# Pools change places at the seam between projection and mixing, and one head's loads change queue

## The chip, the core and the metric

The kernel runs on one core of a Trainium2 chip. The metric is the device time of one execution in microseconds; three runs of a kernel give a median. The traces come from one profiled execution. TensorE (PE) multiplies matrices, VectorE (DVE), ScalarE (ACT) and GpSimd (POOL) work on tiles, SyncE (SP) issues most DMAs. Each engine takes its instructions strictly in the order in which they stand in its own program and waits on semaphores where one depends on another engine or on a DMA.

## What is computed

One layer of a streaming encoder is run for two request groups with the same weights: 1024 first frames of a new stream, and 32 further frames of a running one, which the kernel puts side by side into 1056 columns. Cut to what matters:

```
mod = silu(c) @ w_ada + b_ada                      # adaLN: shift, scale, gate
h = x * (1 + sc1) + sh1
mq,mk,mv,mo,mi,mf, fq,fk,fv,ff, gu,gv = split(h @ w_in)
hm = head_norm(mlstm(mq, mk, mv, ...)) * norm_g * sigmoid(mo)
hf = softmax(fq @ fk.T + decay(ff), causal) @ fv   # 8 heads of 64
hg = spatial_gate(gu, layer_norm(gv))
mix = concat([hm, hf, hg]) @ w_o
x = layer_norm(ALPHA * x + (1 + g1) * mix) * ln1_g + ln1_b
h = x * (1 + sc2) + sh2
y = (silu(h @ w_gate) * (h @ w_up)) @ w_down       # D_FF = 2816
x = layer_norm(ALPHA * x + (1 + g2) * y)
```

The softmax of a new stream runs over its whole past; the running stream brings a cache of 256 keys per head.

## The kernel before

**Arithmetic.** Products are taken in fp32 accuracy from rounded halves: each operand is split into a high part and a low remainder, and a product is three matmuls, high by high, high by low, low by high (`gemm`, L110). `weights` (L92) brings a weight block into `raw` by SP's queue, ScalarE makes the high half (L104, `whi`), VectorE the low one (L105, `wlo`).

**Columns and stages.** Model columns 0 to 511 are group 0, the rest group 1. Phase 1 projects everything and writes q, k, v, gates and so on to scratch arrays in DRAM (`dqh`, `dql`: high and low halves of q and k of each head; `dv`, `dmqk`, `dmv`, `dmo`; `dfs`: the forget decay; `dM`). Group 0's attention is done in phase 1. Then come group 0's output projection (`wo`), its first layer norm (`ln1`) and, for the last three heads, group 1's q and k (`fm_unit` with `evac_qk(h, True)`). In `evac_qk` (L358) ScalarE and VectorE write the halves into the small tiles `qkh` and `qkl`, SP stores them to `dqh` and `dql`, and the exact k goes from `qkr` to the output `o_kT` on ScalarE's own DMA queue. `ln1_res(0)` (L1094) rescales the residual `z[0]` on GpSimd (L1101), 16 tiles.

**The seam.** After that two pools are released (`s1.close()`): `p1`, with group 1's projection input in halves (`h1h`, `h1l`) and some constants, and `sm`, with the small tiles. Both lie on the right side of the on-chip memory; `sm` was opened second. The pool `mx1` is opened on the same side and takes their addresses. A tile of `mx1` may be written only when the last readers of what lay there are done; for a tile that was being stored, when the store has landed.

**What follows.** `mixers` (L1322) runs, for heads 0 to 7, the second phase of the attention (`fox`, L737: queries of tiles 4 to 7), woven with the mLSTM blocks (`mlstm`, L584; the first of them beside head 1 in the order of the program's text), and, before head 1, the running stream's attention (`fox_sample`). `fox` loads per head `qp` (q high and low), `k1` (k high, twice), `q2` and `k2` (with decay rows, `decay` L381) and `v`, all by SP's queue; the first two matmuls on them are L779 and L780 (`fox_s`). `mlstm` loads `mqk`, `mqb`, `mv1`, `mo` and `mb`; `mqb` and a column of `mv1` are first set by GpSimd (L594, L599); ScalarE then takes the sigmoid of `mo` in three steps (L607 to L609) and VectorE reads `mb` (L615). The feed-forward part of group 0 is written behind the mixers: `up` (L1122) multiplies the normed columns (`tm_ah`, `tm_al`) by gate and up weights into `up_g` tiles, takes silu in three ScalarE steps (L1139 to L1141) and two VectorE products (L1142, L1143) and splits the result. Pieces of adaLN (`ada`, L170: products L178, a copy by ScalarE L181, transposes L184, a sum L186) stand between.

**What sets the order.** The program's text is only the start: when the kernel is built, a scheduler that simulates a timeline puts the instructions into their final order on each engine, keeping dependencies, and interleaves `up`, `ada` and `mixers`. `issue_after(x)` forbids an instruction to be placed ahead of x.

Of the kernel before, what the change touches and what calls it, by code (L numbers as in the profile page):

```python
# [63 lines left out]
def f(ap):  # L64
    return ap.bitcast(F32)


class Kernel:
# [12 lines left out]
        kw = {} if bufs is None else {"bufs": bufs}  # L81
        return pool.tile(shape, dt, tag=tag, name=f"{self.phase}_{tag}_{self.n}", **kw)

    def load(self, out, in_):
        self.lastload = self.nc.sync.dma_start(out, in_)
        return self.lastload

# [290 lines left out]
                    nc.gpsimd.tensor_copy(self.qks[:, h, :], kr[:, n - NS:n])  # L378
        return evac

    def decay(self, out, h, rows, tiles):  # L381
        j0, j1 = tiles
        self.load(f(out).rearrange("p (j q) -> p j q", q=P),
                  self.dfs.rearrange("(j h) r q -> h r j q", h=8)[h, rows, j0:j1])

    def head_tiles(self, h, nq, nk):
        b = self.foxbufs
# [349 lines left out]
    def fox(self, h, chunks):  # L737
        self.phase = "fox"
        mx = self.mx
        q0, q1 = chunks[0][0] * P, (chunks[-1][-1] + 1) * P  # L740
        nq, nk, nb = q1 - q0, q1, q1 // P
        if h in self.heads:
            k1, k2, qp, q2, v = self.heads.pop(h)
        else:
            k1, k2, qp, q2, v = self.head_tiles(h, nq, nk)
            qs = slice(q0, q1)
            self.load(f(qp[0:64]), self.dqh[h, 0:64, qs])
            self.load(f(qp[64:128]), self.dql[h, 0:64, qs])
            self.load(f(k1[0:64]), self.dqh[h, 64:128, :nk])
            self.load(f(k1[64:128]), self.dqh[h, 64:128, :nk])  # L750
            self.load(f(q2[0:64]), self.dqh[h, 0:64, qs])
            self.decay(q2[64:68], h, slice(2, 6), (chunks[0][0], nb))
            self.load(f(k2[0:64]), self.dql[h, 64:128, :nk])
            self.decay(k2[64:68], h, slice(0, 4), (0, nb))
            self.load(f(v), self.dv[:, :nb, h * P:(h + 1) * P])
        for tiles in chunks:
            o = tiles[0] * P - q0
            n = len(tiles) * P
            yield from self.fox_chunk(h, tiles, nk, n, k1, k2, qp[:, o:o + n], q2[:, o:o + n], v)
# [405 lines left out]
    def sup_operand(self, ks):  # L1165
# [7 lines left out]
        def load(k):  # L1173
# [5 lines left out]
            return x, y  # L1179

        loaded = {k: load(k) for k in ks[:2]}
        yield
        for k in ks:
            self.phase = "sup"
            x, y = loaded.pop(k)
            tt(y[:, b], y[:, b], x[:, b], ALU.subtract)
            tt(x[:, b], x[:, a], x[:, b], ALU.subtract)
            tt(x[:, a], y[:, b], x[:, a], ALU.add)
            tt(y[:, a], x[:, a], y[:, a], ALU.subtract)
            for z, (h, l) in zip((x, y), self.T):  # L1190
                nc.scalar.copy(h[:, k], z)
                tt(l[:, k], z, f(h[:, k]), ALU.subtract)
            if k + 2 in ks:
                loaded[k + 2] = load(k + 2)
            yield
# [141 lines left out]
    def run(self):  # L1337
        nc, tc, d = self.nc, self.tc, self.d
# [25 lines left out]
        self.constants()  # L1364
        self.ph = self.pool("ph")
        s1 = ExitStack()
        self.p1 = self.pool("p1", ctx=s1, side="right")
        self.sm = self.pool("sm", 2, ctx=s1, side="right")
        self.h1t = [self.wide_tiles(), [self.t(self.p1, [P, KT, GN[1]], F32R, x) for x in ("h1h", "h1l")]]
        self.hs = self.t(self.p1, [P, KT, 2 * NS], F32R, "hs")  # L1370
        self.G = self.t(self.p1, [P, 9, 16], F32, "G")
# [97 lines left out]
        weave(self.ln1(0, st, *MM[0][1]))  # L1469
        for h in range(PRE, 8):  # L1470
            self.fm_unit(w3[2 + h], self.evac_qk(h, True), (1,))
        self.ln1_res(0)
        s1.close()
        s4 = ExitStack()
        self.mx = self.pool("mx1", ctx=s4, side="right")
        self.foxbufs = (2, 1, 1, 1, 2)
        self.mixers()
        s5 = ExitStack()
        pa = self.pool("pa0", ctx=s5)
        self.pu, self.utag = self.pg, "gg"  # L1480
# [78 lines left out]
        for half, (a, b) in enumerate(LN[1][::-1]):  # L1559
# [6 lines left out]
            else:  # L1566
                h, l = (self.t(pb, [P, KT * 272], F32R, f"{x}{a}", 1) for x in ("ah", "al"))
# [117 lines left out]
```

## Time and profile before

| | us |
|---|---|
| runs, median (lowest to highest, three) | 1366.96 (1365.69 to 1368.74) |
| profiled execution | 1366.61 |
| span of its trace, first to last instruction | 1364.7 |
| mean granted TensorE clock | 0.995 of full speed |

The profile's page begins with the busy time of each engine. The granted clock tells at what share of full speed TensorE was allowed to run. In a timeline the columns are start, duration, engine, line, operation, output and inputs, tile shape, and in brackets the idle time ahead of it and what ended it; the names of DMAs that an engine issues stand under a queue (SPq, ACTq). The names in the trace carry the phase: `fox_qp` is head 0's qp here, `fm_qkr` the small tile of group 1's projection, `up_whi` a weight half, `start_dqh` a scratch array. The windows table gives for a stretch the busy time and count of PE, its weight loads, DVE, ACT and POOL, then the clock, the share of the 16 DMA engines that is busy, and GB/s.

### The profile page before, as it was taken

How to read it: one execution, taken by the hardware profiler on the slowest of the kernel's cores; microseconds unless marked ns; L12 is line 12 of the kernel's file. 1: busy time of each engine (PE TensorE's matmuls, PEld its weight loads, DVE VectorE, ACT ScalarE, POOL GpSimd, SP SyncE). 2: the span in 40 equal slices, each digit the busy share in tenths (PEclk: the TensorE clock that was granted, in tenths of full speed). 3: DMA queues.
4: the chain of work that ended last, by engine and by line, in shares of the span. 5: the costliest groups of instructions: out<-in, count | busy, mean ns of one | idle time of the engine just before them, and what ended most of it. 6: DMA issues, size and time to landing. Idle time of an engine off the chain costs nothing.

```text
span 1364.7 us, 25185 instructions
## 1 busy us (share of the span) xinstructions
PE 1330.3 (97%) x9434; PEld 1215.8 (89%) x9434; DVE 995.4 (73%) x2129; ACT 656.7 (48%) x1306; POOL 226.6 (17%) x263
## 2 busy tenths in 40 slices
PE   7999999999999899999999999999999999999996
PEld 4898889998989777888887888999999999999995
DVE  5545553679769667786776765678988988879777
ACT  3314454545536554545545354336664554645355
POOL 0202000053134200000000000373710000000341
PEclk9999999999999899999999999999999999999998
DMA  9765565547454765454344334574596758454321
GB/s 359 273 231 152 161 206 154 163 138 212 134 201 135 207 189 171 119 154 134 109 122 120 104 110 130 156 181 124 164 254 170 205 149 223 146 170 127 99 79 66
DMA packets 119289, 221.70 MB, mean 162 GB/s; under 512 B 18676, under 2 KB 62352, under 8 KB 119168
## 3 DMA queue, kind: packets, MB, share of 16 engines
q1 hardware_dynamic: 111936, 207.55, 48.9%
q0 software_dynamic: 6032, 11.94, 5.1%
q8 instruction: 74, 1.21, 0.4%
q10 hardware_dynamic: 1200, 0.62, 0.2%
q14 instruction: 47, 0.39, 0.1%
HBM read 188.13 MB, written 51.85 MB: 176 GB/s over the span
## 4 chain that ended last, share of the span: by engine, by line
PE 84%; DVE 7%; DMA 5%; ACT 2%; issue 1%; SPq 1%; POOL 1%; DVEq 0%; ACTq 0%
PE up_g L117 5%; PE up_g L118 5%; PE up_g L116 5%; PE dn_g L116 4%; PE dn_g L118 4%; PE dn_g L117 4%; PE tm_g L281 3%; PE tm_g L282 3%; PE tm_g L283 3%; PE sup_u L118 3%; PE sup_u L116 3%; PE sup_u L117 3%; PE fox_t L815 2%; PE sup_g L117 2%; PE sup_g L118 2%; PE sup_g L116 2%
## 5 line engine op out<-in xcount | busy, mean ns | idle before, releaser
L117 PE MATMUL up_g<-tm_al,up_whi 128*128 128x512 f32 (+1 forms) x384 | 141.0, 367 | 0.5 <-DVE tm_al L1092 0.5
L116 PE MATMUL up_g<-tm_ah,up_whi 128*128 128x512 f32 (+1 forms) x384 | 141.2, 369 | 0.2
L118 PE MATMUL up_g<-tm_ah,up_wlo 128*128 128x512 f32 (+1 forms) x384 | 140.5, 366 | 0.0
L1211 ACT CAST sup_whi<-sup_raw 128x1024 fp32r<-128x1024 f32 x54 | 56.0, 1048 | 90.3 <-PE dn_u L117 46.7
L116 PEld LDWEIGHTS up_g<-tm_ah,up_whi 128*128 128x128 f32 x384 | 72.7, 190 | 12.5 <-ACT tm_ah L1091 0.6
L117 PEld LDWEIGHTS up_g<-tm_al,up_whi 128*128 128x128 f32 x384 | 73.1, 190 | 11.1 <-DVE tm_al L1092 0.7
L118 PEld LDWEIGHTS up_g<-tm_ah,up_wlo 128*128 128x128 f32 x384 | 73.2, 191 | 10.7
L788 ACT ACTIVATE fox_p<-fox_s,fox_fmx 128x384 f32<-128x384 f32 (+2 forms) x96 | 55.1, 578 | 44.8 <-DVE fox_fmx L786 37.4
L104 ACT CAST up_whi<-up_raw 128x1024 fp32r<-128x1024 f32 x50 | 52.4, 1048 | 49.7 <-PE up_g L117 19.0
L1212 DVE TENSOR_TENSOR sup_wlo<-sup_raw,sup_whi 128x1024 fp32r<-128x1024 f32 x54 | 68.2, 1267 | 10.5 <-ACT sup_whi L1211 10.5
L1066 DVE SCALAR_TENSOR_TENSOR wo_z<-dn_g,start_mod,wo_z 128x512 f32<-128x512 f32 (+4 forms) x120 | 60.3, 521 | 20.1 <-PE dn_g L118 19.7
L105 DVE TENSOR_TENSOR up_wlo<-up_raw,up_whi 128x1024 fp32r<-128x1024 f32 x50 | 65.7, 1314 | 11.6 <-ACT up_whi L104 11.0
L116 PE MATMUL dn_g<-up_acth,dn_whi 128*128 128x512 f32 (+2 forms) x200 | 74.1, 371 | 0.0
L118 PE MATMUL dn_g<-up_acth,dn_wlo 128*128 128x512 f32 (+2 forms) x200 | 73.4, 367 | 0.0
L117 PE MATMUL dn_g<-up_actl,dn_whi 128*128 128x512 f32 (+2 forms) x200 | 72.9, 365 | 0.0
L820 ACT CAST fox_pth<-fox_t 128x512 fp32r<-128x512 f32 (+1 forms) x80 | 41.0, 545 | 59.5 <-PE fox_t L815 59.3
L104 ACT CAST dn_whi<-dn_raw 128x1024 fp32r<-128x1024 f32 (+1 forms) x44 | 42.7, 971 | 52.2 <-PE up_g L117 10.7
L783 DVE TENSOR_REDUCE fox_fmx<-fox_s 128x1 f32<-128x384 f32 (+2 forms) x96 | 52.7, 553 | 13.0 <-PE fox_s L780 11.8
L821 DVE TENSOR_TENSOR fox_ptl<-fox_t,fox_pth 128x512 fp32r<-128x512 f32 (+1 forms) x80 | 49.5, 631 | 14.5 <-ACT fox_pth L820 14.4
L105 DVE TENSOR_TENSOR dn_wlo<-dn_raw,dn_whi 128x1024 fp32r<-128x1024 f32 (+1 forms) x44 | 49.5, 1125 | 13.7 <-ACT dn_whi L104 13.2
L281 PE MATMUL tm_g<-tm_whi,start_h1h 128*128 128x256 f32 (+1 forms) x192 | 55.3, 288 | 1.7 <-ACT tm_vhl L711 1.7
L282 PE MATMUL tm_g<-tm_wlo,start_h1h 128*128 128x256 f32 (+1 forms) x192 | 55.1, 287 | 0.0
(667 smaller groups left out, 4806.8 us busy)
## 6 DMA issues: line engine op xcount, KB each, us to landing
up_raw<-w_gu SPq DMA_DIRECT2D x50, 512.0 KB
dn_raw<-w_dn SPq DMA_DIRECT2D x28, 512.0 KB
ada_late<-w_ada SPq DMA_DIRECT2D x24, 512.0 KB
sup_raw<-w_gu SPq DMA_DIRECT2D x20, 512.0 KB
start_dp<-w_gu SPq DMA_DIRECT2D x19, 512.0 KB
start_dp<-w_gu POOLq DMA_DIRECT2D x19, 512.0 KB, 7.5
wo_raw<-w_o SPq DMA_DIRECT2D x18, 512.0 KB
sup_raw<-start_dp SPq DMA_DIRECT2D x18, 512.0 KB
```

The costliest lines, as they stand in the source:

```text
L104: nc.scalar.copy(hi[:, :w], raw[:, :w])
L105: (eng or nc.vector).tensor_tensor(lo[:, :w], raw[:, :w], f(hi[:, :w]), ALU.subtract)
L116: nc.tensor.matmul(ps, hi, xh(k), start=start and k == 0, stop=False)
L117: nc.tensor.matmul(ps, hi, xl(k), start=False, stop=False)
L118: nc.tensor.matmul(ps, lo, xh(k), start=False, stop=stop and k == n - 1)
L281: nc.tensor.matmul(ps[:, :ncol], xh, hi, start=k == 0, stop=False)
L282: nc.tensor.matmul(ps[:, :ncol], xh, lo, start=False, stop=False)
L783: nc.vector.tensor_reduce(mxs[:, x:x + 1], s[:, :w], AX.X, ALU.max, negate=True)
L788: nc.scalar.activation(pr[:, lo:hi], banks[x][:, :hi - lo], AF.Exp, bias=mxs[:, 0:1], accum_out=sums[:, x:x + 1])
L1066: self.lastz = self.nc.vector.scalar_tensor_tensor(z[:, m, x:y], ps[:, x - a:y - a], g[i], z[:, m, x:y], ALU.mult, ALU.add)
L1211: nc.scalar.copy(h, x)
L1212: tt(l, x, f(h), ALU.subtract)
```

## The change

Three edits. The pools `sm` and `p1` are opened in the other order, so `sm` now lies where `p1` began. `load` and `decay` take an engine, and `fox` passes GpSimd for head 0: its eight loads of qp, k1, q2 and k2 go by GpSimd's DMA queue, v stays on SP's. `ln1_res(0)` is called after `mixers`, and may not be placed ahead of the last of these eight loads. Lines below the first edit are 3 to 4 higher in the changed kernel (L779 becomes L783, L607 L610, L184 L187, L1142 L1146).

```diff
@@ -81,7 +81,10 @@
         kw = {} if bufs is None else {"bufs": bufs}
         return pool.tile(shape, dt, tag=tag, name=f"{self.phase}_{tag}_{self.n}", **kw)
 
-    def load(self, out, in_):
+    def load(self, out, in_, eng=None):
+        if eng:
+            self.lastside = eng.dma_start(out, in_)
+            return self.lastside
         self.lastload = self.nc.sync.dma_start(out, in_)
         return self.lastload
 
@@ -378,10 +381,10 @@
                     nc.gpsimd.tensor_copy(self.qks[:, h, :], kr[:, n - NS:n])
         return evac
 
-    def decay(self, out, h, rows, tiles):
+    def decay(self, out, h, rows, tiles, eng=None):
         j0, j1 = tiles
         self.load(f(out).rearrange("p (j q) -> p j q", q=P),
-                  self.dfs.rearrange("(j h) r q -> h r j q", h=8)[h, rows, j0:j1])
+                  self.dfs.rearrange("(j h) r q -> h r j q", h=8)[h, rows, j0:j1], eng)
 
     def head_tiles(self, h, nq, nk):
         b = self.foxbufs
@@ -744,14 +747,15 @@
         else:
             k1, k2, qp, q2, v = self.head_tiles(h, nq, nk)
             qs = slice(q0, q1)
-            self.load(f(qp[0:64]), self.dqh[h, 0:64, qs])
-            self.load(f(qp[64:128]), self.dql[h, 0:64, qs])
-            self.load(f(k1[0:64]), self.dqh[h, 64:128, :nk])
-            self.load(f(k1[64:128]), self.dqh[h, 64:128, :nk])
-            self.load(f(q2[0:64]), self.dqh[h, 0:64, qs])
-            self.decay(q2[64:68], h, slice(2, 6), (chunks[0][0], nb))
-            self.load(f(k2[0:64]), self.dql[h, 64:128, :nk])
-            self.decay(k2[64:68], h, slice(0, 4), (0, nb))
+            eng = self.nc.gpsimd if h == 0 else None
+            self.load(f(qp[0:64]), self.dqh[h, 0:64, qs], eng)
+            self.load(f(qp[64:128]), self.dql[h, 0:64, qs], eng)
+            self.load(f(k1[0:64]), self.dqh[h, 64:128, :nk], eng)
+            self.load(f(k1[64:128]), self.dqh[h, 64:128, :nk], eng)
+            self.load(f(q2[0:64]), self.dqh[h, 0:64, qs], eng)
+            self.decay(q2[64:68], h, slice(2, 6), (chunks[0][0], nb), eng)
+            self.load(f(k2[0:64]), self.dql[h, 64:128, :nk], eng)
+            self.decay(k2[64:68], h, slice(0, 4), (0, nb), eng)
             self.load(f(v), self.dv[:, :nb, h * P:(h + 1) * P])
         for tiles in chunks:
             o = tiles[0] * P - q0
@@ -1364,8 +1368,8 @@
         self.constants()
         self.ph = self.pool("ph")
         s1 = ExitStack()
+        self.sm = self.pool("sm", 2, ctx=s1, side="right")
         self.p1 = self.pool("p1", ctx=s1, side="right")
-        self.sm = self.pool("sm", 2, ctx=s1, side="right")
         self.h1t = [self.wide_tiles(), [self.t(self.p1, [P, KT, GN[1]], F32R, x) for x in ("h1h", "h1l")]]
         self.hs = self.t(self.p1, [P, KT, 2 * NS], F32R, "hs")
         self.G = self.t(self.p1, [P, 9, 16], F32, "G")
@@ -1469,12 +1473,13 @@
         weave(self.ln1(0, st, *MM[0][1]))
         for h in range(PRE, 8):
             self.fm_unit(w3[2 + h], self.evac_qk(h, True), (1,))
-        self.ln1_res(0)
         s1.close()
         s4 = ExitStack()
         self.mx = self.pool("mx1", ctx=s4, side="right")
         self.foxbufs = (2, 1, 1, 1, 2)
         self.mixers()
+        with tc.issue_after(self.lastside.ins):
+            self.ln1_res(0)
         s5 = ExitStack()
         pa = self.pool("pa0", ctx=s5)
         self.pu, self.utag = self.pg, "gg"
```

The scheduler's order is the same up to the seam. There it changes as follows. On SP's queue, from the last weight load ahead of the seam on, before:

```order
L85 DMA up_raw_7987<-w_gu 128x1024
L85 DMA fox_qp_5839<-start_dqh_57 64x512
L85 DMA fox_qp_5839<-start_dql_58 64x512
L85 DMA fox_k_1018_5837<-start_dqh_57 64x1024 x2
L85 DMA fox_q_1021_5840<-start_dqh_57 64x512
L85 DMA fox_q_1021_5840<-start_dfs_64 4x4x128
L85 DMA fox_k_1019_5838<-start_dql_58 64x1024
L85 DMA fox_k_1019_5838<-start_dfs_64 4x8x128
L85 DMA fox_v_5841<-start_dv_59 128x8x128
L85 DMA foxs_k_1071_6032<-cache_k 64x1024
```

and now, with head 0's loads gone and the mLSTM block's drawn forward:

```order
L88 DMA up_raw_7987<-w_gu 128x1024
L88 DMA fox_v_5825<-start_dv_59 128x8x128
L88 DMA foxs_k_1071_6016<-cache_k 64x1024
L88 DMA mlstm_mqk_6144<-start_dmqk_60 128x4x128
L88 DMA mlstm_mv_1103_6150<-start_dmv_61 128x4x64
L88 DMA foxs_k_1071_6016<-start_dsf_65 1x4x256
L88 DMA mlstm_mo_6153<-start_dmo_62 128x256
L88 DMA mlstm_mb_6155<-start_dM_66 128x512
```

Head 0's v and the first mLSTM block's loads stand directly behind the weights; `mqb` follows five rows behind `mb`. The eight loads stand on GpSimd behind the residual's additions (L1065) and ahead of the first mLSTM block's settings and the residual's 16 rescalings (L1105).

On ScalarE (the casts of `tm_ah` are the last of the layer norm, `mo` is the mLSTM block's sigmoid, `up_sil_7892` the silu of `up_g_7900`, `ada_adas` adaLN's copy) it stood before:

```order
L1091 CAST tm_ah_4639<-lna_tmp_5587 128x256
L181 COPY ada_adas_7970<-ada_g_7957 128x256
L104 CAST up_whi_7989<-up_raw_7987 128x1024
L1139 ACTIVATE up_sil_7892<-up_g_7900 128x256
L1140 ACTIVATE up_sil_7892<-up_sil_7892,start_ones_36_112 128x256
L1141 ACTIVATE up_sil_7892<-up_sil_7892 128x256
L788 ACTIVATE fox_p_5853,fox_fsm_5852<-fox_s_5854,fox_fmx_5851 128x384
L788 ACTIVATE fox_p_5853,fox_fsm_5852<-fox_s_5858,fox_fmx_5851 128x256
L607 ACTIVATE mlstm_mo_6169<-mlstm_mo_6169 128x256
L1144 CAST up_acth_7828<-up_sil_7892 128x256
```

and stands now:

```order
L1095 CAST tm_ah_4639<-lna_tmp_5587 128x256
L610 ACTIVATE mlstm_mo_6153<-mlstm_mo_6153 128x256
L611 ACTIVATE mlstm_mo_6153<-mlstm_mo_6153,start_ones_36_112 128x256
L107 CAST up_whi_7989<-up_raw_7987 128x1024
L1143 ACTIVATE up_sil_7892<-up_g_7900 128x256
L612 ACTIVATE mlstm_mo_6153<-mlstm_mo_6153 128x256
L621 ACTIVATE mlstm_mw_6192<-mlstm_mw_6192,start_col_178 128x128 x4
L1144 ACTIVATE up_sil_7892<-up_sil_7892,start_ones_36_112 128x256
L184 COPY ada_adas_7970<-ada_g_7957 128x256
L1145 ACTIVATE up_sil_7892<-up_sil_7892 128x256
```

The sigmoid on `mo` has come to stand directly behind the layer norm's last cast, and adaLN's copy behind `mw`. On TensorE the first `fox_s` pair and what follows it stood before among the matmuls on `up_g_7900` and `up_g_7925`, whose last 16 come behind it:

```order
L118 MATMUL up_g_7925<-tm_ah_4639,up_wlo_7839 128x256
L116 MATMUL up_g_7925<-tm_ah_4639,up_whi_7838 128x256
L779 MATMUL fox_s_5854<-fox_k_1018_5837,fox_qp_5839 128x384
L779 MATMUL fox_s_5858<-fox_k_1018_5837,fox_qp_5839 128x256
L117 MATMUL up_g_7900<-tm_al_4640,up_whi_7832 128x256
L118 MATMUL up_g_7900<-tm_ah_4639,up_wlo_7833 128x256
L117 MATMUL up_g_7925<-tm_al_4640,up_whi_7838 128x256
```

and now all matmuls on these two are ahead of it:

```order
L119 MATMUL up_g_7925<-tm_ah_4639,up_whi_7838 128x256
L120 MATMUL up_g_7925<-tm_al_4640,up_whi_7838 128x256
L121 MATMUL up_g_7925<-tm_ah_4639,up_wlo_7839 128x256
L181 MATMUL ada_g_7957<-ada_raw_7964,start_c_63_182 32x256 x4
L783 MATMUL fox_s_5838<-fox_k_1018_5821,fox_qp_5823 128x384
L783 MATMUL fox_s_5842<-fox_k_1018_5821,fox_qp_5823 128x256
L187 MATMUL ada_g_7957<-start_ident_121,ada_adas_7970 128x128 x2
L119 MATMUL up_g_7993<-tm_ah_4639,up_whi_7983 128x512
L120 MATMUL up_g_7993<-tm_al_4640,up_whi_7983 128x512
L121 MATMUL up_g_7993<-tm_ah_4639,up_wlo_7984 128x512
```

Behind the pair stand now adaLN's transposes and `up_g_7993`, which takes the accumulator bank of `up_g_7900` and waits until VectorE's L1146 has read that.

## The prediction

> **What bounds the kernel now.** I read the page's busy table first. TensorE is the bound: the rest of the span is small.
>
> ```profile
> span 1364.7 us, 25185 instructions
> PE 1330.3 (97%) x9434; PEld 1215.8 (89%) x9434; DVE 995.4 (73%) x2129; ACT 656.7 (48%) x1306; POOL 226.6 (17%) x263
> ```
>
> TensorE stands idle for 34.4 us. The view of what each engine waited for names one wait that belongs to this change, and the same view of SyncE's queue (440 to 475 us) names what that wait comes from:
>
> ```profile
> PE fox_s L779 <- DMA fox_k<-start_dqh: 4.2, 1, 4.2
> SPq L85 <- DMA o_kT<-fm_qkr: 3.4, 1, 3.4
> ```
>
> The timelines of PE, ACT and SP show the place, at the seam where phase 1 ends and head 0's second phase begins:
>
> ```profile
> 444.50 0.29 PE L118 MATMUL fm_g<-start_h1h,fm_wlo 128*128 128x272 f32 x1
> 449.94 0.48 ACTq L89 DMA_DIRECT2D o_kT<-fm_qkr  x1
> 454.06 0.47 SPq L85 DMA_DIRECT2D fox_qp<-start_dqh  x1
> 456.58 0.28 PE L118 MATMUL up_g<-tm_ah,up_wlo 128*128 128x256 f32 x1
> 456.70 0.28 PE L116 MATMUL up_g<-tm_ah,up_whi 128*128 128x256 f32 x1
> 461.21 0.87 PE L779 MATMUL fox_s<-fox_k,fox_qp 128*128 128x384 f32 x2 [4.23 <-DMA fox_k<-start_dqh]
> 465.72 0.65 PE L780 MATMUL fox_s<-fox_k,fox_q 68*128 68x384 f32 x2
> 466.21 0.40 PE L116 MATMUL up_g<-tm_ah,up_whi 128*128 128x512 f32 x1
> ```
>
> Head 0's operands lie where the small tiles qkr, qkh and qkl lay, so the first load (fox_qp) waits until the last store of qkr has landed: issued at 449.94, landed at 454.06, that is 4.1 us. TensorE has meanwhile run out of work, at 456.98. Up to there a 128x256 matmul started every 0.12 us (456.58 to 456.70); after the wait the clock has fallen. The table by windows has it, with the granted clock third from the end, then the DMA engines' share and GB/s:
>
> ```profile
> 444.80:450.00 5.20, 5.20 (x46) 5.20 (x46) 5.20 (x14) 3.83 (x8) 1.37 (x1) 1.00 0.45 160
> 450.00:454.06 4.06, 3.38 (x23) 2.76 (x23) 3.41 (x10) 4.06 (x12) 4.06 (x6) 1.00 0.54 146
> 454.06:457.00 2.94, 2.92 (x31) 1.99 (x29) 2.83 (x6) 2.37 (x7) 2.94 (x4) 1.00 0.23 52
> 457.00:461.20 4.20, 0.00 (x0) 0.02 (x1) 0.00 (x0) 0.00 (x0) 0.81 (x2) 0.77 0.96 234
> 461.20:466.20 5.00, 4.99 (x22) 5.00 (x23) 0.54 (x3) 0.88 (x1) 0.00 (x0) 0.51 1.06 210
> 466.20:470.00 3.80, 3.80 (x19) 3.07 (x18) 3.08 (x8) 2.37 (x8) 0.00 (x0) 1.00 1.15 276
> ```
>
> So the stall costs 4.23 us of idling and 5.0 x 0.49 = 2.45 us of slow clock: **6.7 us is all that this change can win**.
>
> **What the change does here.** After it head 0's tiles lie over group 1's operand (h1h), whose last reader is the matmul at 444.50, and the loads stand on GpSimd's queue. They can start some 9 us earlier than at 454.06. Issue and landing there are known from GpSimd's own transfers:
>
> ```profile
> 128.17 0.98 POOL L89 DMA_DIRECT2D start_dfs<-gates_mqk  x2
> 354.53 0.57 POOL L89 DMA_DIRECT2D o_kT<-fm_qkr  x1 [0.29 <-POOL fm_qkr L370]
> start_dvn<-tm_traw POOLq DMA_DIRECT2D x8, 128.0 KB, 4.3
> start_dfs<-gates_mqk POOLq DMA_DIRECT2D x2, 64.0 KB, 5.3
> ```
>
> An issue takes 0.5 (0.98 for two) to 0.57 us, so the eight are out by about 449.5, and they land, at 4.3 to 5.3 us each, by about 455. TensorE's order has moved too: the 16 matmuls on up_g that stood behind the first fox_s now stand ahead of it. They take 16 x 0.12 = 1.9 us from 456.8, and with four adaLN products and the pair of fox_s TensorE would be through at about **459.4**, with no wait for head 0. That wait is gone.
>
> What is late next is the other half of the swap. The mLSTM block's tiles (mqb, mv, mo, mb) now lie over qkr, qkh and qkl, so the load of mv on SP's queue takes over the wait for the landing at 454.06, with mo behind it. And ScalarE's order has moved: the sigmoid on mo now stands directly behind the last tm_ah, ahead of the weight cast, the silu of up_g and the copy of ada_adas. ScalarE takes its work in order, so it stands still until mo has landed, and TensorE's next two things need what is behind: the adaLN transposes read the copy, and up_g_7993 takes the accumulator bank that DVE frees by its product of up_g_7900 and the silu.
>
> Spacings on SP's queue, and a landing there:
>
> ```profile
> 461.06 0.67 SPq L85 DMA_DIRECT2D foxs_k<-start_dsf  x1
> 461.83 0.59 SPq L85 DMA_DIRECT2D mlstm_mqk<-start_dmqk  x1
> 463.82 0.59 SPq L85 DMA_DIRECT2D mlstm_mv<-start_dmv  x1
> 464.46 0.49 SPq L85 DMA_DIRECT2D mlstm_mo<-start_dmo  x1
> 466.11 0.33 SPq L85 DMA_DIRECT2D mlstm_mb<-start_dM  x1
> 470.02 0.69 DVE L615 TENSOR_TENSOR mlstm_mw<-mlstm_mb,start_maskbig 128x512 f32<-128x512 f32 x1 [0.66 <-DMA mlstm_mb<-start_dM]
> ```
>
> mv at 454.06, dsf 0.64 later (463.82 to 464.46), mo 0.77 later (461.06 to 461.83): mo is issued at 455.5. mb took 3.9 us to land (466.11 to 470.0), the qkr store 4.1. The lower bound for mo's landing M is therefore 455.5 + 4.1 = 459.6. The upper one comes from the DMA engines. The windows give what they carried anyway from 444.8 to 457: 0.45 x 5.20 + 0.54 x 4.06 + 0.23 x 2.94 = 5.2 us of full engines; and what head 0's loads, v, the cache and the mLSTM loads took in before: 0.96 x 4.20 + 1.06 x 5.00 = 9.3 us. All that now lies before M. At the highest share seen, 1.15, 14.5 us of it take 12.6 us, so from 444.8 to 457.4 at the earliest; the first 2 us run at 0.45 only, which makes it 458.6, and some 3 us of landing at the tail give 461.5. I take M = **460.3**, nearer to the rows of single landings, because the 3.9 us of mb were measured with the engines full.
>
> ScalarE's work from M on, each by the distance to the next start in before:
>
> ```profile
> 456.06 0.36 ACT L181 COPY ada_adas<-ada_g 128x256 f32<-128x256 f32 x1
> 465.32 1.05 ACT L104 CAST up_whi<-up_raw 128x1024 fp32r<-128x1024 f32 x1 [8.89 <-PE up_g L117]
> 466.27 0.38 ACT L1139 ACTIVATE up_sil<-up_g 128x256 f32<-128x256 f32 x1
> 466.68 0.51 ACT L1140 ACTIVATE up_sil<-up_sil,start_ones 128x256 f32<-128x256 f32 x1
> 467.23 0.42 ACT L1141 ACTIVATE up_sil<-up_sil 128x256 f32<-128x256 f32 x1
> 470.03 0.41 ACT L607 ACTIVATE mlstm_mo<-mlstm_mo 128x256 f32<-128x256 f32 x1
> 470.34 0.40 ACT L1144 CAST up_acth<-up_sil 128x256 fp32r<-128x256 f32 x1
> 470.63 0.51 ACT L608 ACTIVATE mlstm_mo<-mlstm_mo,start_ones 128x256 f32<-128x256 f32 x1
> 471.04 1.27 ACT L618 ACTIVATE mlstm_mw<-mlstm_mw,start_col 128x128 f32<-128x128 f32 x4
> 472.21 0.41 ACT L609 ACTIVATE mlstm_mo<-mlstm_mo 128x256 f32<-128x256 f32 x1
> 468.49 0.41 DVE L1142 TENSOR_TENSOR up_sil<-up_g,up_sil 128x256 f32<-128x256 f32 x1
> ```
>
> mo 0.31, its second step 0.41, the cast 0.95, silu's first step 0.41, mo's third step about 0.31 (as its first), mw 1.17, silu's second step 0.55, the copy 0.36: 4.5 us, so the transposes run at M + 4.5 = 464.8. Silu's third step 0.42 and DVE's product 0.41 make it M + 5.3: up_g_7993 starts at **465.6**. DVE's own extra, mw behind mb (issued some 0.6 us after mo) and the lower half of the weights, is done before M + 4.9 and is covered by ScalarE's chain; if mb came over 2 us after mo it would not be.
>
> TensorE is idle from 459.4 to 464.8, longer than the 4.2 us after which the clock was down. So I charge the same recovery: 5.0 us at 0.51 from 464.8, of which 465.6 to 469.8 hit up_g_7993: 4.2 x 0.49 = 2.06 us. The second pair of fox_s, done before 466.21 in before, is still to do: 0.65 x 0.51 = 0.33. In full-speed terms TensorE stands at 465.6 + 2.06 + 0.33 = 468.0 where it stood at 466.2: **+1.8 us**. With M at 459.6 it is +1.1, at 461.5 +3.0.
>
> In sentences apart: the Trainium skill, "TensorE: Matmul & The Clock Gate", Part 1 (The HAM clock gate), puts both the idle window and the busy one at about 3.4 us. The fall agrees with the 0.77 of the idle window here; the return took 5.0 us here. By its 3.4 us the slow stretch would end at 468.2 and the sum would be +1.0; the row decides.
>
> **ln1's rescaling** moves behind the loads on GpSimd:
>
> ```profile
> L1101 POOL TENSOR_SCALAR wo_z<-wo_z,start_colp 128x256 f32<-128x256 f32 (+1 forms) x32 | 34.7, 1092 | 26.0 <-ACT lna_tmp L1087 26.0
> ```
>
> Sixteen of these are 17.5 us. They hide behind TensorE's up matmuls of group 0: their first reader, the residual of the down projection, comes only when those are through. Without that cover they would cost up to their own 17.5 us. The memsets of mqb and mv also stand behind the loads, but SP's mv does not wait for them. The swap by itself costs nothing else that I can find: the busy row has TensorE at 97%, and once the seam is passed weights are loaded earlier than in before.
>
> The sum goes against the profiled execution, 1366.61 us (its span of 1364.7 and 1.9 around it): 1368.4. The median of the three runs, 1366.96, is 0.35 above it, so I forecast **1368.8 us**.
>
> **The rivals.**
> (a) The stall simply disappears: ScalarE is not held because mo lands early. For this 5.3 us of chain would have to end by 459.4, so mo in place at 454.1, and the landing at 454.06 alone forbids it. Part of the way is possible where the qkr store lands sooner. Full gain 6.7, so 1360.3. The Trainium skill's page "DMA: Bandwidth & Descriptors", section "Anatomy of one DMA — SWDGE (gpsimd) path", gives about 2.0 us plus bytes over 436 GB/s: the store would land at 452.1 and mo at about 455.8, so up_g_7993 at 461.1, a gap too short for the clock to fall and an estimate of 1362.2 by that page; the 4.1 and 3.9 us measured here are against it. What a row can still bear is a small gap without the slow clock. Chance 0.15.
> (b) On the other side: the DMA engines choke between 446 and 458. In before, the seam had 0.45 to 0.54 of them taken, and the 9.3 us of loads ran after it at 0.96 to 1.15. Now the loads fall into it; both the qkr store and mo land later, and each us of either is a us of TensorE. It decides from M = 461.2 on, where the sum passes +2.7. With the store late by 1 and mo by 1.2, M = 462.5: +4.0, **1371.0**. For it speak the shares; against it that mb landed in 3.9 us under the same load. Chance 0.25.
> (c) The change doesn't do what it says: the software queue is slow, and fox_s waits all the same. It matters only past 464.6, 20 us after the first issue; at 467 it would add 2.4, 1371.2. Against it speak landings of 4.3 to 5.3 us. Chance 0.06.
>
> **How the numbers follow.** Forecast 0.54, (a) 0.15, (b) 0.25, (c) 0.06. What this kernel's runs can tell from no change is about 0.2%, 2.7 us. The forecast's own range, 1367.5 to 1369.7, is all within that; (a) is faster, (b) and (c) are slower: 0.15, 0.54, 0.31. For the range I reach into (a) down to 1361.5 and over (b) up to 1372.5.
>
> **What would show it.** Right: no wait of TensorE on fox_k; instead a wait of 5 to 6 us, by ada_t or up_g on ScalarE or DVE, near 459 to 465; ScalarE idle before the first step on mo, released by the DMA of mo; SP's mv at 454; a window at a clock of about 0.5 behind it. Wrong: TensorE busy through 455 to 470, ScalarE's mo before 456, or a wait at fox_s on GpSimd's loads; a DMA share above 1 from 447 on with the landing of the qkr store past 455 would be (b).

## The result, and the profile after

The changed kernel takes 1373.67 us (median of 14 runs, 1370.96 to 1376.43), the kernel before beside it 1366.82 us (14 runs, 1362.54 to 1370.42): 1.0052 times as long, 95% interval 1.0043 to 1.0061. That is 6.85 us lost, where 1.8 were forecast. The profiled execution is one of 1373.19 us.

The head of the changed kernel's page, and two rows of its table of waits (engine, line and instruction, what it waited for, us in total, times, longest):

```profile
span 1371.4 us, 25201 instructions
PE 1334.0 (97%) x9434; PEld 1215.7 (89%) x9434; DVE 998.5 (73%) x2129; ACT 657.0 (48%) x1306; POOL 224.0 (16%) x271
```

```profile
PE ada_g L187 <- ACT ada_adas L184: 6.8, 1, 6.8
PE up_g L119 <- DVE up_sil L1146: 0.6, 1, 0.6
```

No wait of TensorE on `fox_k` is left. In its place stand 6.8 us ahead of the adaLN transposes, which read ScalarE's copy `ada_adas`, and 0.6 on the product with `up_sil`. The timeline of TensorE at the seam:

```profile
459.63 0.64 PE L181 MATMUL ada_g<-ada_raw,start_c 128*32 128x256 f32 x8
460.20 0.55 PE L783 MATMUL fox_s<-fox_k,fox_qp 128*128 128x384 f32 x2
467.51 0.69 PE L187 MATMUL ada_g<-start_ident,ada_adas 128*128 128x128 f32 x2 [6.76 <-ACT ada_adas L184]
468.29 0.79 PE L119 MATMUL up_g<-tm_ah,up_whi 128*128 128x512 f32 x1
```

Head 0's scores run at 460.20 without a wait; then TensorE stands until 467.51. ScalarE (and its queue), SyncE's queue and GpSimd in the same stretch:

```profile
450.37 0.47 ACTq L92 DMA_DIRECT2D o_kT<-fm_qkr  x1
463.16 0.42 ACT L610 ACTIVATE mlstm_mo<-mlstm_mo 128x256 f32<-128x256 f32 x1 [6.57 <-DMA wo_tmp<-start_dmix]
467.11 0.35 ACT L184 COPY ada_adas<-ada_g 128x256 f32<-128x256 f32 x1
```
```profile
456.76 0.38 SPq L88 DMA_DIRECT2D mlstm_mv<-start_dmv  x1
457.95 0.42 SPq L88 DMA_DIRECT2D mlstm_mo<-start_dmo  x1
```
```profile
449.18 0.64 POOL L86 DMA_DIRECT2D fox_k<-start_dfs  x1
456.82 0.52 POOL L597 MEMSET mlstm_mqb<- 128x512 f32 x1 [7.01 <-DMA o_kT<-fm_qkr]
```

The last store of qkr goes out at 450.37 and is through at 456.8: GpSimd's memset of mqb is released by it, and SyncE's load of mv stands at 456.76. The load of mo follows at 457.95, and the sigmoid on mo starts at 463.16, 5.2 us later (the bracket names another DMA that ended at about that time; the instruction reads only mo). From there ScalarE works through what is queued behind, and the copy comes at 467.11. Windows over the seam, and one over the stretch of the slow clock alone (columns as before):

```profile
445.00:450.40 5.40, 5.40 (x48) 5.40 (x47) 5.40 (x15) 3.70 (x8) 4.37 (x8) 1.00 0.87 244
450.40:456.80 6.40, 5.24 (x38) 3.80 (x37) 5.42 (x15) 6.19 (x17) 0.00 (x0) 1.00 1.03 271
456.80:460.00 3.20, 3.20 (x34) 2.82 (x30) 0.31 (x1) 0.00 (x0) 3.17 (x7) 1.00 1.17 207
460.00:463.10 3.10, 0.75 (x10) 0.30 (x2) 0.00 (x0) 0.00 (x0) 3.10 (x7) 0.89 1.14 326
```
```profile
462.43:472.67 10.24, 5.07 (x12) 3.76 (x13) 4.70 (x10) 6.03 (x14) 5.86 (x8) 0.50 0.70 224
```

The DMA engines, 0.45 to 0.54 busy here in the kernel before, are full from 450 on (1.03 to 1.17), and the clock is at half speed for 10.24 us, 5.16 of them after TensorE has work again. The last matmul on `fm_g`, ahead of all that the change moves, starts at 444.85 in this trace and at 444.50 in the one before; from there to the end of the span it is 926.5 us here and 920.2 there, 6.35 more.

### The profile page after: what moved, and what is told of

It reads as the page before. It is cut to its first block, busy times and chain, and to the rows that moved or that the text cites. A ratio compares the mean times of both kernels' runs of the same rounds, so it can differ in the third digit from the quotient of the medians.

```text
span 1371.4 us, 25201 instructions
## 1 busy us (share of the span) xinstructions
PE 1334.0 (97%) x9434; PEld 1215.7 (89%) x9434; DVE 998.5 (73%) x2129; ACT 657.0 (48%) x1306; POOL 224.0 (16%) x271
## 4 chain that ended last, share of the span: by engine, by line
PE 89%; DVE 5%; DMA 4%; ACT 1%; issue 1%; SPq 0%; POOL 0%; DVEq 0%; ACTq 0%
PE up_g L119 6%; PE up_g L120 6%; PE up_g L121 6%; PE dn_g L119 4%; PE dn_g L121 4%; PE dn_g L120 4%; PE tm_g L284 3%; PE tm_g L285 3%; PE tm_g L286 3%; PE sup_u L121 3%; PE sup_u L119 3%; PE sup_u L120 3%; PE fox_t L819 2%; PE fm_g L119 2%; PE fm_g L120 2%; PE sup_g L120 2%
```

## The experiments

Each run stands beside runs of the kernel before on the same chip; a ratio is against those, with its 95% interval, which reaches 1.2 to 2.4 us to each side. No runs of the change stand beside them, so a difference of 2 us between a run and the change is at the edge of what the times can tell.

**The swap alone** (before, with only the pools exchanged).

```
+        self.sm = self.pool("sm", 2, ctx=s1, side="right")
         self.p1 = self.pool("p1", ctx=s1, side="right")
-        self.sm = self.pool("sm", 2, ctx=s1, side="right")
```

> Only the pools change places; head 0's loads stay on SP's queue and ln1's rescaling stays where it was. The built order on every engine is that of before at the seam. Seam theory (the time is set by what TensorE waits for there): head 0's first load no longer waits for the store of qkr (454.06 in before) but only for the last reader of h1h, so it goes out right behind the weight load at 450.0, 3.7 us earlier; the first fox_s is ready near 457.5, TensorE idles under 1 us, the clock does not fall: 5 to 6.5 us faster than before, about 1361. Rival (the swap itself costs, since the mLSTM tiles now lie over the small tiles): 1367 or more.

1367.39 us, ratio 1.0000 (0.9988 to 1.0012). The waits of TensorE between 444 and 520 us in its trace:

```profile
PE fox_s L779 <- DMA foxs_k<-start_dsf: 2.2, 1, 2.2
PE up_g L117 <- DVE tm_al L1092: 1.1, 1, 1.1
PE fox_t L815 <- DVE fox_p L796: 1.1, 1, 1.1
PE fox_o L823 <- DVE fox_ptl L821: 0.9, 1, 0.9
PE up_g L116 <- ACT up_whi L104: 0.6, 1, 0.6
```

The swap alone cuts the wait at head 0 from 4.2 to 2.2 us, the clock does not fall, and the first 512-wide product on up_g comes 3.6 us sooner after the last fm_g than before (18.1 against 21.7). Expected were 5 to 6.5 us of time, and none came: most of the gain is lost again in small waits behind it (1.1, 0.9 and 0.6 us in the rows, and 0.4 on `up_wlo`; the one on `tm_al` stands ahead of head 0). Removing the stall is not the same as winning its length.

**The change without the swap**, and **the change with ln1's rescaling in its old place**.

```
         self.p1 = self.pool("p1", ctx=s1, side="right")
+        self.sm = self.pool("sm", 2, ctx=s1, side="right")
```
```
             self.fm_unit(w3[2 + h], self.evac_qk(h, True), (1,))
+        self.ln1_res(0)
         s1.close()
...
-        with tc.issue_after(self.lastside.ins):
-            self.ln1_res(0)
```

> The changed kernel with the pools in their old places: GpSimd's queue and the late rescaling without the swap. Head 0's loads wait for the landing of the qkr store again, ScalarE's order is that of the changed kernel. Seam theory: without the loads ahead of it the store lands near 454 (6.4 us after issue in the changed kernel, 4.1 in before), the loads reach their tiles near 460 to 462, mo lands near 458 to 459; TensorE idles 2 to 4 us from 459.4, up_g_7993 starts near 464 to 465 instead of 468.3: 3 to 4 us faster than the changed kernel, 1369 to 1371, of which about 2 us are the adaLN products in nine groups instead of four. Rival (the swap is what makes the changed kernel slow): 1367 or less. Rival (GpSimd's queue is slow by itself): 1373 or more.

> The changed kernel with ln1's rescaling back in its old place in the text: eleven of the rescalings stand ahead of head 0's loads on GpSimd, so these start near 453 to 454 and the crowding of the DMA engines between 446 and 454 is gone. Seam theory: the qkr store lands near 454.5, mo near 459, head 0's operands near 460 to 462; up_g_7993 near 464.5, 3 to 4 us faster than the changed kernel: 1369 to 1371. Rival (the late rescaling costs by itself): 1367 or less. Rival (neither crowding nor rescaling matters): 1373 to 1375.

1377.99 us, 1.0087 (1.0071 to 1.0103), and 1379.75 us, 1.0099 (1.0082 to 1.0117), where the seam theory had 1369 to 1371 for both. Without the swap TensorE has both waits, and mo lands 13.4 us after its issue; the rows are of its waits, its queue and ScalarE:

```profile
PE ada_g L187 <- ACT ada_adas L184: 5.8, 1, 5.8
PE fox_s L783 <- DMA fox_k<-start_dqh: 5.3, 1, 5.3
```
```profile
454.52 1.08 SPq L88 DMA_DIRECT2D mlstm_mo<-start_dmo  x1
```
```profile
467.93 0.42 ACT L610 ACTIVATE mlstm_mo<-mlstm_mo 128x256 f32<-128x256 f32 x1 [11.47 <-DMA mlstm_mo<-start_dmo]
```

This trace also speaks for what makes the store late in the change. SyncE sends the same loads ahead of mv here, but head 0's eight loads have not begun: the store, issued at 450.23, is through by 452.79, when GpSimd sends the first of them. That is 2.6 us at most, against 6.4, and the DMA engines are 0.39 busy in this time, against 1.03 (GpSimd, and a window; the bracket names another wait of the same instruction):

```profile
452.79 0.55 POOL L86 DMA_DIRECT2D fox_qp<-start_dqh  x1 [36.22 <-ACT tm_ah L1095]
```
```profile
450.30:452.30 2.00, 1.32 (x9) 0.92 (x9) 1.79 (x6) 2.00 (x7) 0.00 (x0) 1.00 0.39 66
```

The store lands early, as the theory had it, and yet nothing is won, because head 0's loads and mo then travel together. Whether GpSimd's queue is slow by itself in such a crowd, the second rival, is not separated by these runs.

With the rescaling early, the last three of its instructions that stand ahead of head 0's loads on GpSimd run from 448.50 on, and the loads start there at 452.86 and not at 445.44; the trace has the same pair of waits (5.5 and 4.9). So the late place is what lets the loads go early: without it the change is 6.1 us slower still. That the rescaling itself costs nothing there is read from the change's trace, where no wait of TensorE names it.

**qkr of the last heads in a pool of its own**, so that the mLSTM tiles do not wait for its store: in the change, in before, and in the change with the two order edges of the next experiment.

```
-            kr = self.t(self.sm, [P, 272], F32, "qkr", 2)
+            kr = self.t(self.krp if act else self.sm, [P, 272], F32, "qkr", 2)
```

> The changed kernel with qkr of the last three heads in a pool of its own that outlives the seam, so that nothing waits for the landing of the last qkr store. All else as in the change; the built order at the seam is nearly the same, with adaLN's products in six groups. Seam theory: the load of mo goes out 3 to 4 us earlier, near 454, lands near 458 to 459 in the crowd, ScalarE starts 4 us earlier than 463.2: 4 to 6 us faster than the changed kernel, 1367.5 to 1370. Rival (ScalarE's wait for mo is not what holds TensorE): 1373 or more.

> The kernel before with only qkr in a pool of its own: head 0's loads, on SP's queue, no longer wait for the store of qkr but for that of qkh, some 4 us earlier. Theory: fox_s is ready 3 to 4 us earlier, TensorE idles under 1 us there and the clock stays up; by the swap alone the gain was then taken back by small waits, so 1363 to 1367. Rival (the stall is worth its full 6.7 us): 1360 to 1361.

> The change with qkr in a pool of its own and with mo and mb behind silu as in the run of the edges of order. Theory: no wait for a store's landing and no hold; TensorE waits at most 2 us at the seam; 1361 to 1366. Rival (weights are the next bound, since their load stands behind the mLSTM loads on SP's queue here): 1366 to 1370, with waits on up_raw through ScalarE's cast.

1371.63 us, 1.0037 (1.0024 to 1.0050); 1369.71 us, 1.0020 (1.0009 to 1.0030); 1369.63 us, 1.0018 (1.0007 to 1.0029). In the first, mo is issued at 452.48 and in use at 460.27, 2.9 us earlier than in the change, and TensorE's wait for the copy falls from 6.8 to 2.6 us; 2.0 us of time are won, less than the 4 to 6 expected, and the rest goes to waits on `tm_al` (1.9) and on a later head's operands (1.4). In the other two the separate pool makes the kernel slower than it is without, where 1363 to 1367 and 1361 to 1366 were expected: it lets the mLSTM loads in ahead of the weights, and TensorE waits for the same copy (2.4 us in the second, 5.2 in the third). That the store's landing is what mo waits for is shown; that giving it room is a remedy is not.

**Two order edges**: the change, with the sigmoid on mo put behind silu's third step on ScalarE and the first read of mb behind silu's second product on VectorE. In the second run only mo is moved.

```
+        x = nc.scalar.activation(mo[:L], mo[:L], AF.Exp, scale=-1.0)
+        x = nc.vector.tensor_tensor(w[:L, :, :L], mb[:L, :, :L], ...
...
+            if self.held and a > 0:
+                for x, last in zip(self.held, (y, z)):
+                    self.tc.add_manual_dep(x, last.ins.name, ...
```

> The changed kernel with two edges of order added: the first step of the sigmoid on mo stands behind silu's third step on ScalarE, and the read of mb behind silu's second product on VectorE. Loads, queues, pools and the amount of work are those of the change. Theory (ScalarE and VectorE, held by mo and mb, hold TensorE): the wait of 6.8 us at adaLN's transposes is gone, the clock does not fall, adaLN's products stand in five groups: at least 6 us faster than the changed kernel, 1362 to 1367; small waits on weights further on may take part of it back, as they did with the swap alone. Rival (TensorE is held by the crowded DMA engines whatever stands ahead on ScalarE, by head 0's operands or by the weights): the wait moves to fox_s or to up_g on a weight half and the time stays at 1371 or more.

> As the run before, but only the sigmoid on mo is put behind silu's third step; the read of mb on VectorE and the four steps on mw on ScalarE stay ahead of silu's second step. Theory: mb lands about 1 us after mo, so the hold stays, now by mb through VectorE's mw: TensorE waits 5 to 7 us again, 1371 to 1375. Rival (mo alone is what holds): 1363 to 1368.

Both edges: 1366.38 us, 0.9991 (0.9982 to 1.0000), 7.3 us under the change. mo alone: 1373.8 us in a single run, nothing won: VectorE then stands on mb (its `mlstm_mw` idles 7.12 us for `mb`) and TensorE still waits 6.4 us for the copy. So what the change loses at the seam is in-order engines standing on the mLSTM loads, ScalarE and VectorE alike; 1.7 of the 7.3 us can have another cause, which comes to light further on (TensorE's adaLN products). With both edges the first 512-wide product comes 16.6 us after the last fm_g, 5.1 sooner than before, and most of that is lost again some fifteen us later, where the weights come late (TensorE, then ScalarE):

```profile
478.00 0.79 PE L120 MATMUL up_g<-tm_ah,up_whi 128*128 128x512 f32 x1 [2.73 <-DVE up_sil L1151]
```
```profile
474.26 1.04 ACT L108 CAST up_whi<-up_raw 128x1024 fp32r<-128x1024 f32 x1 [6.62 <-DMA up_raw<-w_gu]
```

**Head 0's v behind mo and mb** on SyncE's queue: 0.5 MB less in flight while the store and mo travel. The load of `foxs_k`, which stood between mv and mo, comes behind mo here too.

```
+        if j == 4:
+            for x in self.big:
+                self.tc.add_manual_dep(x, ld.ins.name, ...
```

> The changed kernel with one edge of order: head 0's v (0.5 MB) is loaded behind mo and mb on SP's queue instead of ahead of them; ScalarE's order still has mo ahead. Theory (the landing of the qkr store and of mo, and with it TensorE's wait, is set by the bytes in the DMA engines): 0.5 MB less ahead at some 260 GB/s lets the store land 1 to 2 us earlier than 6.4 us after its issue and mo 1.5 to 2.5 us earlier; TensorE waits 4.5 to 5.5 us instead of 6.8: 1371 to 1372.5. Rival (the store is slow for another reason, such as GpSimd's issuing): landing 6 us or more after issue, 1373 to 1375.

1371.69 us (five runs, 1370.77 to 1374.30), 1.0043 (1.0030 to 1.0055), 2.0 us under the change by the medians, with intervals that overlap. ScalarE with its queue, and SyncE's queue, in its trace:

```profile
450.56 0.47 ACTq L92 DMA_DIRECT2D o_kT<-fm_qkr  x1
...
460.77 0.42 ACT L614 ACTIVATE mlstm_mo<-mlstm_mo 128x256 f32<-128x256 f32 x1 [3.84 <-issue]
```
```profile
455.88 0.38 SPq L88 DMA_DIRECT2D mlstm_mv<-start_dmv  x1
456.35 0.46 SPq L88 DMA_DIRECT2D mlstm_mo<-start_dmo  x1
```

The store is through 5.3 us after its issue (6.4 in the change) and mo is in use 4.4 after its own (5.2). By themselves these two do not show much: in the other traces that keep the change's loads ahead of them (both edges, mo alone, weights ahead, products in blocks, head 1) the store takes 5.6 to 7.3 us and mo, where ScalarE stands idle for it, 4.4 to 6.1. Together with the earlier place of mo they do: mo is in use 15.6 us after the last fm_g, in those traces and the change 17.5 to 18.7. TensorE's wait for the copy falls from 6.8 to 3.4 us, and the first 512-wide product comes 2.5 us sooner (20.9 against 23.4); 2.1 us are lost again at 519 on a later head's operands. How much of the 2.0 us of time comes from the landings stays open, since this edit regrouped the adaLN products too, as the next experiment tells.

**The next weights ahead**: the run with both edges, and the swap alone with both edges, each with one weight load put ahead of the second mLSTM block's loads and `wo_tmp` on SyncE.

```
+                    for x in self.behind:
+                        self.tc.add_manual_dep(x, ld.ins.name, ...
...
-                with tc.issue_after(self.lastz.ins):
+                with tc.issue_after(self.lastz.ins), tc.issue_after(self.upload.ins):
```

> The run with mo and mb behind silu, and on SP's queue the next weight load (up_raw of the third unit) put ahead of the second mLSTM block's mqk and mb and of group 1's wo_tmp, 0.5 MB that stood ahead of it. In the run before it, that weight load was issued at 466.5 and landed 7.7 us later, ScalarE's cast of it held silu, and TensorE waited 2.7 us at 478 and lost 3.4 us of clock. Theory (the gain at the seam went into that wait): the weights land 2 us earlier, the wait at 478 is under 1 us and the clock stays up: 4 to 6 us faster than with the first two edges, 1360.5 to 1363. Rival (the DMA engines are full, so that the wait only moves to another load): 1365 to 1367.

> The swap alone (loads on SP's queue, rescaling in its old place), with the same order on SP's queue: the next weights ahead of the second mLSTM block's loads and wo_tmp, and mo and mb behind silu. Theory: the seam's stall shrinks as with the swap alone (2.2 us, no fall of the clock), and the small waits of 2 to 3 us on weights that took the gain back shrink: 1362 to 1366. Rival (those waits are not of this weight load): 1366 to 1368, as the swap alone.

1367.68 us, 1.0006 (0.9997 to 1.0015), and 1364.92 us, 0.9990 (0.9981 to 0.9999). In the first the waits between 444 and 520 us are 1.3, 1.0, 0.9 and 0.4, the clock stays full, and yet it is no faster than the kernel before. TensorE is busy in its place: the adaLN products of this stretch, 32 with two records each in the trace, stand in four blocks of 16 records in before and are spread in nine pieces in the change and in this run. Windows of these instructions alone, for before, the change and this run in this order (PE and its weight loads, clock, DMA share, GB/s):

```profile
440.00:530.00 90.00, 4.28 (x64) 1.67 (x64) 0.96 0.66 189
```
```profile
440.00:530.00 90.00, 6.53 (x64) 1.82 (x64) 0.94 0.65 182
```
```profile
440.00:530.00 90.00, 6.94 (x64) 2.03 (x64) 1.00 0.68 193
```

And three more of the pieces in the change, beside the one of eight at 459.63 above, each with the start of what follows (TensorE's timeline):

```profile
481.95 0.63 PE L181 MATMUL ada_g<-ada_raw,start_c 128*32 128x256 f32 x6
482.52 0.44 PE L783 MATMUL fox_s<-fox_k,fox_qp 128*128 128x384 f32 x1
...
483.42 0.62 PE L181 MATMUL ada_g<-ada_raw,start_c 128*32 128x256 f32 x4
483.98 0.44 PE L819 MATMUL fox_t<-start_ident,fox_p 128*128 128x128 f32 x2
...
497.88 1.05 PE L181 MATMUL ada_g<-ada_raw,start_c 128*32 128x256 f32 x10
498.86 0.38 PE L827 MATMUL fox_o<-fox_ptl,fox_v 128*128 128x256 f32 x1
```

Four, six or eight records take the same 0.56 us to the next start, ten take 0.98; a block of 16 takes 1.00 in before (478.41 to 479.41). The nine pieces (seven of up to eight, two of ten) make 5.9 us start to start, the four blocks 4.0: 1.9 us that no wait shows. The starts of the single records show where most of it lies. The four products of one half of a tile, which write 32 rows each of one bank, start within 0.02 us of each other, and their second records 0.2 us later, again together. A piece of six goes as three and three, one of four as two and two, one of ten as four, four, one and one. A half that is cut in two thus takes as many steps in each part as a whole one: 22 steps in the nine pieces, 16 in the four blocks. At some 0.2 us a step that is an estimate of 1.3 of the 1.9 us; the rest comes with the five more pieces, 0.1 us at the end of each.

Other edits regroup these products too. Start to start they take 4.2 us with both edges, 5.2 with mo alone, 4.8 with qkr apart in the change and 5.7 in before, 4.1 with v behind, 6.3 in this run. So up to 1.7 us of what both edges win against the change, 1.2 of qkr apart and 1.8 of v behind can lie in the products and not in what the edit was made for, and qkr apart in before loses up to 1.7 there.

The second run, the swap alone with the same edges, keeps three of the four blocks whole and cuts the fourth once (start to start 4.5 us), and waits 2.0 us in all between 444 and 520 us: 2.0 us under the kernel before, just clear of its interval.

**The products in blocks again**: the first of these two, with four order edges that hold each tile's adaLN products together.

```
+                if u in TARGET and half == 0:
+                    self.tc.add_manual_dep(x.ins, self.mark[TARGET[u]].name, ...
```

> The kernel of the run before this with the weights ahead, in which TensorE waits for nothing of note behind the seam, and yet no faster than before; its 64 adaLN products stand in pieces of 8, 8, 10, 6, 10 and so on between other products, and start to start they take 6.3 us there, 4.0 us in before and 4.5 us in the swap with the weights ahead, where they stand in four blocks of 16. Here four order edges on TensorE put them into four blocks of 16 again; nothing else is edited. Theory (products in pieces cost TensorE time by themselves, some 2 us of the change's loss): the products take some 4.3 us, and the time falls by about 2 us, to 1365.7. Rival (the pieces only fill time that TensorE would lose anyway): the products take less, others more, and the time stays at 1367.7 within 0.7.

1368.32 us, 1.0004 (0.9990 to 1.0019): by the time alone the rival, since nothing is won. The trace shows the products back at the figure of before and a new wait later on (windows of the products, then VectorE, SyncE's queue and TensorE at head 1):

```profile
440.00:530.00 90.00, 4.28 (x64) 1.67 (x64) 0.98 0.67 193
```
```profile
501.71 0.41 DVE L859 TENSOR_TENSOR fox_fo<-fox_o,fox_fo 64x256 f32<-64x256 f32 x1
```
```profile
502.24 0.50 SPq L96 DMA_DIRECT2D start_dmix<-fox_fo  x1
502.84 0.55 SPq L92 DMA_DIRECT2D fox_k<-start_dqh  x1
```
```profile
510.22 0.53 PE L802 MATMUL fox_s<-fox_k,fox_qp 128*128 128x384 f32 x2 [3.76 <-DMA fox_k<-start_dqh]
```

TensorE comes to head 1's scores 60.8 us after the last fm_g, where before needs 64.8, and stands there: head 1's operands are queued on SyncE behind the store of head 0's output, which VectorE finishes at 502.1.

**Head 1's operands ahead of that store**: the same, with two more order edges on SyncE (the store, and the second load of the down projection's weights, behind head 1's operands).

```
+                    for x in (self.st0x, ld):
+                        self.tc.add_manual_dep(x.ins, self.q1.ins.name, ...
```

> The kernel of the run before this, with its adaLN products in four blocks, plus two order edges on SyncE: the store of head 0's first output and the second load of the down projection's weights stand behind head 1's operands. In the run before, those operands were issued from 502.8 on, right behind that store, which went out when VectorE had written fox_fo (501.71 + 0.41), and TensorE, which reached head 1's scores 60.4 us after the last fm_g (64.8 in before), waited 3.8 us for them and then had a slow clock: 5.4 us, about what had been won ahead. Theory (the time won at the seam is real and is lost at the next transfer that is too late): the wait at head 1 goes, and the time falls by 3 to 5.4 us, to 1363 to 1365, under both kernels. Rival (the loss moves on once more, to the weights or the next head): within 1 us of 1368.3.

1363.64 us (12 runs, 1360.70 to 1367.16) against 1367.65: 0.9974 (0.9962 to 0.9985), the fastest version of all, 4.0 us under before and 10 under the change. The waits of TensorE between 444 and 520 us, and SyncE's queue:

```profile
PE up_g L136 <- DVE up_sil L1179: 0.8, 2, 0.6
PE up_g L137 <- DVE tm_al L1127: 0.4, 1, 0.4
PE fox_t L848 <- DVE fox_p L829: 0.2, 1, 0.2
```
```profile
497.45 1.58 SPq L93 DMA_DIRECT2D fox_k<-start_dqh  x2
...
501.58 0.46 SPq L97 DMA_DIRECT2D start_dmix<-fox_fo  x1
```

Counted from the last fm_g the operands go out 3.1 us earlier than in the run before (54.1 against 57.2), nothing waits at head 1, and the time of the seam is kept. Against the run with the weights ahead, 4.0 us are won; the traces show the products in blocks (2.3 us less start to start) and 2.2 us less of small waits. The same two edges on SyncE without the blocks were not tried; that run has no wait at head 1 beyond 0.4 us for them to remove.

## Why the prediction was wrong

**Right:** the place and the kind. TensorE no longer waits for head 0, GpSimd's issues are out at 449.8 (449.5 was said), and the wait moves to the adaLN transposes and up_g behind ScalarE standing on mo. The two edges confirm it by time, even if 1.7 of their 7.3 us are set apart for the products. ScalarE's chain was said to be M + 4.5 and M + 5.3 and is 4.35 and 5.13; the clock was charged with 5.0 us at 0.51 after the gap and was at 0.50 for 5.16. No wait of TensorE names ln1's rescaling where it stands now.

**The step that failed is M**, the landing of mo: "I take M = 460.3, nearer to the rows of single landings". It was 463.1, or 462.8 when both traces are counted from the last fm_g, which starts 0.35 us later here: 2.5 us late. The sum took over the landing of the qkr store from before, 454.06, unchanged, though the change sends head 0's loads ahead of and beside it; it came at 456.76. mo itself took 5.2 us where 4.8 were allowed. Each us of M is a us of TensorE. Even the upper bound of 461.5 was too low: it counted 14.5 us of full engines to be carried before M, and the windows above give 0.87 x 5.40 + 1.03 x 6.40 + 1.17 x 3.20 + 1.14 x 3.10 = 18.6 between 445 and 463.1. The case that was met is rival (b), which decides from 461.2 on; its two signs, a share above 1 and the store past 455, are both there. Its mechanism is shown for the store by three traces (at most 2.6 us with the engines 0.39 busy, without the swap; 4.1 at 0.54, before; 6.4 at 1.03, in the change), and for mo by the run with v behind: there mo is in use 15.6 us after the last fm_g, where the forecast's M stood at 15.8 and the change has 18.3. What this is worth in time is read from TensorE's timeline, not from that run's median.

**The term that was missing** is the order of TensorE's own products. The prediction looked at TensorE's order at the seam and named the four adaLN products there, and did not see that they had been cut off from their other four, there and at the next three tiles. That is 1.9 us start to start. 1.8 forecast, 2.5 for M and 1.9 for the pieces are 6.2 of the 6.35 us between the two traces. This is a sum of two traces; no run gives the time of the pieces alone, because in the run with the blocks the next transfer took it back. Rival (b) alone, with the M that came, gives 1371.3, so no case that was written reached the measured time, and the range ended 1.2 us below it.

**Half right:** "6.7 us is all that this change can win" took it that a stall removed is time won. The swap alone and the two edges each take TensorE 3.6 and 5.1 us ahead and win nothing or next to nothing, because the loads behind the stall used it as their own slack. The stall of before hid three later ones: the weights, head 1's operands, and the small waits between. Part of it was to be had only with them out of the way: 2.0 us with the weights, 4.0 with all of them.

## What to carry to other kernels

Before a load is moved earlier, add up what else will be in flight with it, and take the landing of every transfer in that stretch, those that are not touched too, from rows measured under such a load, not from the quiet stretch that it has now. An instruction that reads a late transfer belongs behind everything on its engine that the busiest engine needs; an order that the scheduler gives should be read for this first, on every engine, and for blocks of like products that it has cut up. And where a stall goes, ask for the next transfer that used its time: the gain is only as long as that one's slack.

## What the runs showed of the hardware

**The slow clock comes in whole steps.** In before it is 6.83 us long, in the change 10.24, in the run with the products in blocks some 3.4 (0.88 in 3 us and 0.67 in 4 us around 512): two, three and one times 3.41. The Trainium skill, "TensorE: Matmul & The Clock Gate", Part 1, has a free-running window of about 3.4 us, and these lengths agree with it. How much of a slow stretch falls on work differs: in the change 5.16 of the 10.24 us did.

**A landing is no property of a transfer.** The same load of mo was in use 5.2, 7.8 and 13.4 us after its issue (the change, qkr apart, no swap), and the same store was through after at most 2.6 us with the DMA engines 0.39 busy, after 4.1 at 0.54, and after 5.6 to 7.3 us with head 0's loads and v ahead of it. Even with the same loads ahead, one trace differs from the next by up to 1.7 us.

**Cutting a group of small products costs steps.** Four adaLN products of 32 rows start within 0.02 us of each other; cut in two, each part takes the two steps that the whole takes, and the same 64 records cost 5.9 us in nine pieces and 4.0 in four blocks.

**The same program starts unevenly.** The last two versions differ by two edges at 500 us; in their profiled executions the last fm_g, ahead of anything that the edges touch, starts at 445.63 and 443.38. Stretches were therefore measured from that instruction, and times by medians.
